# Re-ordering the opening of a diffusion-backbone kernel, the weight pieces of its last middle norm, and one convolution chunk

## The chip, the cores and the metric

The program runs on one core of a Trainium2 chip. The metric is the device time of one execution in microseconds (us). TensorE (PE in the profile) multiplies matrices, VectorE (DVE), ScalarE (ACT) and GpSimd (POOL) work elementwise, and SyncE (SP) issues transfers; ACT issues some transfers too. Each engine executes its own instructions in the order in which the program lists them and waits on semaphores where an operand is not there yet.

## The reference, cut to what matters

The reference is a two-layer trunk over 512 tokens of width 1024, all in float32:

```
h  = rmsnorm(x, g1) * (1 + s1) + sh1       # m = silu(c) @ w_mod + b_mod gives s1, sh1, ...
hc = the same for 256 context tokens, with silu(c_ctx)
layer 0: x += gate1 * mixer(h, hc)         # spatial gating beside neighbourhood attention, w_in / w_out
layer 1: x += gate1 * conv_module(h)       # pw1, GLU, 31-tap depthwise conv, layernorm, silu, pw2
both:    x += gate2 * (relu(rmsnorm(x, g2) * (1 + s2) + sh2) @ w1)^2 @ w2
out = rmsnorm(x, final_g)
```

Three places of it matter here. The **opening** is the first norm: sums of squares of x over the 1024 channels, the first quarter of the modulation vector of layer 0 (silu(c) and silu(c_ctx) times 2048 columns of `w_mod`), the modulated operand h, and the first query and key products with `w_in`. The **last middle norm** is the norm in layer 1 between the convolution module's output projection (pw2) and the MLP. The **convolution** works channel block by channel block.

## The kernel before, in words

Activations lie transposed, 128 channels on the partitions and 512 tokens along the free dimension, so x is eight blocks `x0[0..7]`. Every float32 operand of a large product is split in two float32r parts, hi (a rounded copy) and lo (the remainder), and each product is three matmuls: `w_hi·h_hi`, `w_lo·h_hi`, `w_hi·h_lo` (lines 88, 89 and 90, helper `mm3`). Weights come in tiles of 1024 x 256 (1 MB). A tile is cut into four **pieces** of two channel blocks each: ACT casts the hi part (line 93), DVE or POOL subtracts to get the lo part (line 94). `W.piece(i, q)` cuts piece q of weight i; `W.pieces(n)` cuts the next n; `W.use()` hands a cut weight out; cutting a weight's last piece issues the load of the next raw tile, which has two buffers.

The order of the work is written out by hand: the engines follow the program's order, and the program only adds the semaphores. Eight completion semaphores serve all transfers in turn.

**Opening (lines 246 to 524).** Transfers are issued first: SP takes `cc`, `x0[0,1]`, `x0[4,5]`, `vec`, `wmA0`, a raw weight, `wmA2`, `wmA3`, the second raw weight, `wmA4` to `wmA7`; ACT takes `x0[2,3]`, `x0[6,7]`, `kon`, `wmA1`. Then ACT computes `sc = silu(cc)` (line 370) while PE runs eight dummy products (`keep_warm`, line 376). ACT squares the eight x blocks (line 383), DVE adds them in pairs (line 385), and PE forms column sums of each pair with a vector of ones: four matmuls (eight instructions) per pair, line 387. The root follows (lines 391, 392). `mod_products(f)`, f = 0 to 3, makes modulation tile f: four products with `wmA[2f]`, four with `wmA[2f+1]` (line 421), an ACT copy `ms` (line 426), four transposes (line 430), and three small DVE operations (lines 435, 437, 438) that give gain and shift of x blocks 2f and 2f+1. `first_operand(f)` then makes hi (ACT, line 464) and lo (DVE, lines 465 and 466) of these two blocks. `first_products(ks, ns)` multiplies blocks ks with column groups ns of the first two weights; column groups 0 and 1 belong to weight 0, groups 2 and 3 to weight 1. In the kernel before, PE does the products of a block well after its operand was made: blocks 2 and 3 between modulation tiles 2 and 3, blocks 4 and 5 after tile 3. After blocks 6 and 7 the sums of squares of the context tokens are made (class `SumSq`: ACT squares at lines 310 and 313, DVE adds at line 321, one product with ones at line 327), and then the value products begin (line 88 with weight tile `w`).

**Convolution (conv_module, lines 1288 to 1437).** `glu(c)` multiplies a gate chunk and a value chunk and writes a padded row block `ypad` (DVE, line 1218); from it shifted copies `y4` are made by 16 transfers on SP (line 1242), for block 7 by 10 transfers and 6 ACT copies (line 1240). `conv_pe(c, t0, t1)` is the depthwise convolution of block c on PE (line 1262), 64 instruction pairs for half of the tokens. `take(c)` adds a finished block to the running sums. `W.pieces` and `work` put weight pieces and left-over vector work between.

**Last middle norm (norm_between, lines 1018 to 1100, called for this place by `lead1`).** PE finishes output chunks 4 and 5 over all tokens, then chunks 6 and 7 over the first 256 tokens, then chunk 6 over the second 256. In the middle of the last one stands the product with ones that totals the squares of the first half (line 327). DVE evacuates each chunk into x (line 1012), ACT squares it (line 313), DVE adds it (line 321). `chunk` puts its weight pieces ahead of its evacuation.

## Time and profile before

| | |
|---|---|
| median of 3 runs | 1176.19 us (1175.85 to 1176.26) |
| the profiled execution's own time | 1176.03 us |
| its span, first to last instruction | 1174.2 us |
| PE busy | 1154.7 us, 98% |
| DVE, ACT, POOL busy | 722.4, 473.9, 170.0 us |
| granted clock, mean over the span | 0.996 |

Matmul ends in the profile are modelled and matmuls overlap, so the time that PE loses is read from the starts of its instructions, and from the idle time that the profile puts ahead of one. "Idle before, <- X" names what ended the wait.

### The profile page before, as it was taken

To read this page: it belongs to the slowest core of one execution; us is meant where nothing else is said; L and a number is where in the kernel's file an instruction comes from. 1 tells how busy PE (TensorE), PEld (TensorE's weight loads), DVE (VectorE), ACT (ScalarE), POOL (GpSimd) and SP (SyncE) were. 2 spreads that over 40 slices of the span, in tenths; PEclk is the share of its full clock that TensorE was granted. 3 is DMA by queue.
4 is the path that set the end of the run, shared out by engine and by line. 5 is a ranking of instruction groups with operands and counts; after the bars stand their busy time and mean duration, and the time that the engine had idled before them with its cause. 6 is when DMAs were issued, how large, how long until landed. Compare 5 with 4: busy or idle time off the path is not lost.

```text
span 1174.2 us, 16562 instructions
## 1 busy us (share of the span) xinstructions
PE 1154.7 (98%) x6620; PEld 959.6 (82%) x6620; DVE 722.4 (62%) x1252; ACT 473.9 (40%) x939; POOL 170.0 (14%) x162
## 2 busy tenths in 40 slices
PE   8999999999999999999999999999999999999997
PEld 4688898889888888888889666698988888888887
DVE  4765778758765665666666878577643443443445
ACT  4474455546431422423336233564632331341423
POOL 0250327533000000000023110143200000000001
PEclk9999999999999999999999999999999999999999
DMA  9624543351554554554541444303232332232322
GB/s 383 228 81 137 188 162 109 126 215 37 215 210 152 212 215 156 203 215 172 186 144 41 151 113 140 99 24 122 72 107 73 108 108 77 103 108 72 108 73 72
DMA packets 31469, 161.91 MB, mean 138 GB/s; under 512 B 4320, under 2 KB 7904, under 8 KB 15008
## 3 DMA queue, kind: packets, MB, share of 16 engines
q1 hardware_dynamic: 27360, 146.09, 35.6%
q10 hardware_dynamic: 4032, 14.76, 3.7%
q8 instruction: 52, 0.85, 0.3%
q14 instruction: 25, 0.20, 0.1%
HBM read 152.52 MB, written 2.10 MB: 132 GB/s over the span
## 4 chain that ended last, share of the span: by engine, by line
PE 87%; DVE 6%; DMA 3%; ACT 2%; issue 1%; POOL 0%; ACTq 0%; DVEq 0%; SPq 0%; POOLq 0%
PE ps L88 23%; PE ps L90 22%; PE ps L89 22%; PE ps L214 4%; PE ps L211 4%; PE ps L212 4%; PE ps L1262 3%; PE ps L892 1%; DMA graw<-in_wmA_dram 1%; DVE graw L557 1%; DMA graw<-in_wmB_dram 1%; PE ps L846 1%; DVE acc L321 1%; PE ps L421 1%; PE ps L876 1%
## 5 line engine op out<-in xcount | busy, mean ns | idle before, releaser
L93 ACT CAST whi<-raw 128x512 fp32r<-128x512 f32 x340 | 191.2, 616 | 199.4 <-PE ps L90 152.3
L88 PE MATMUL ps<-hhi,whi 128*128 128x512 f32 x640 | 251.6, 393 | 1.4 <-DVE gn L743 1.4
L90 PE MATMUL ps<-hlo,whi 128*128 128x512 f32 x640 | 249.3, 390 | 0.6 <-DVE hlo L466 0.6
L89 PE MATMUL ps<-hhi,wlo 128*128 128x512 f32 x640 | 249.4, 390 | 0.2 <-DVE wlo L94 0.2
L94 DVE TENSOR_TENSOR wlo<-raw,whi 128x512 fp32r<-128x512 f32 x284 | 194.7, 723 | 35.6 <-ACT whi L93 34.7
L90 PE MATMUL ps<-hid,whi 128*128 128x512 f32 (+1 forms) x520 | 196.3, 378 | 0.0
L89 PE MATMUL ps<-hid,wlo 128*128 128x512 f32 (+1 forms) x520 | 196.3, 378 | 0.0
L88 PE MATMUL ps<-hid,whi 128*128 128x512 f32 (+1 forms) x520 | 196.3, 378 | 0.0
L1012 DVE SCALAR_TENSOR_TENSOR x<-ps,mod,x 128x512 f32<-128x512 f32 (+1 forms) x94 | 62.7, 668 | 156.8 <-PE ps L90 147.8
L88 PEld LDWEIGHTS ps<-hhi,whi 128*128 128x128 f32 x640 | 120.1, 188 | 32.4 <-issue 5.3
L94 POOL TENSOR_TENSOR wlo<-raw,whi 128x512 fp32r<-128x512 f32 x56 | 81.6, 1473 | 426.9 <-ACT whi L93 426.8
L90 PEld LDWEIGHTS ps<-hlo,whi 128*128 128x128 f32 x640 | 120.1, 188 | 26.1 <-DVE hlo L466 1.0
L89 PEld LDWEIGHTS ps<-hhi,wlo 128*128 128x128 f32 x640 | 120.2, 188 | 24.5 <-DVE wlo L94 0.5
L557 DVE CUSTOM_DVE_ANT_0 graw<-graw,cB,vec 128x1024 f32<-128x1024 f32 x80 | 107.4, 1345 | 15.8 <-DMA graw<-in_wmB_dram 15.8
L88 PEld LDWEIGHTS ps<-hid,whi 128*128 128x128 f32 x520 | 97.8, 188 | 18.2
L89 PEld LDWEIGHTS ps<-hid,wlo 128*128 128x128 f32 x520 | 97.8, 188 | 18.1
L90 PEld LDWEIGHTS ps<-hid,whi 128*128 128x128 f32 x520 | 97.8, 188 | 18.1
L1138 DVE TENSOR_TENSOR z<-z 128x512 f32<-128x512 f32 (+1 forms) x72 | 46.1, 646 | 95.5 <-ACT z L1136 95.5
L1136 ACT ACTIVATE z<-ps 128x512 f32<-128x512 f32 (+1 forms) x72 | 38.9, 550 | 140.6 <-PE ps L90 137.1
L1142 DVE TENSOR_TENSOR hid<-z,hid 128x512 fp32r<-128x512 f32 (+1 forms) x72 | 45.7, 641 | 43.3 <-ACT hid L1140 43.3
L1140 ACT CAST hid<-z 128x512 fp32r<-128x512 f32 (+1 forms) x72 | 40.6, 572 | 51.4 <-DVE z L1138 51.4
L1492 POOL TENSOR_TENSOR o<-o,rstd 128x256 f32<-128x256 f32 x2 | 1.9, 950 | 323.1 <-DVE rstd L332 323.1
(261 smaller groups left out, 1695.4 us busy)
## 6 DMA issues: line engine op xcount, KB each, us to landing
raw<-in_w_ff_dram SPq DMA_DIRECT2D x64, 1024.0 KB
graw<-in_wmB_dram SPq DMA_DIRECT2D x28, 1024.0 KB
graw<-in_wmB_dram ACTq DMA_DIRECT2D x24, 512.0 KB
raw<-in_w_pw_dram SPq DMA_DIRECT2D x12, 1024.0 KB
raw<-in_w_in_dram SPq DMA_DIRECT2D x10, 1024.0 KB
wmA<-in_wmA_dram SPq DMA_DIRECT2D x6, 1024.0 KB
y<-ypad SPq DMA_DIRECT2D x90, 67.5 KB
raw<-in_w_out_dram SPq DMA_DIRECT2D x4, 1024.0 KB
```

Of the source, the lines that this page charges most:

```text
L88: pe.matmul(ps, w[0], a[0], start=first, stop=False)
L89: pe.matmul(ps, w[1], a[0], start=False, stop=False)
L90: pe.matmul(ps, w[0], a[1], start=False, stop=last)
L93: (e or act.copy)(hi, src)
L94: (el or dve).tensor_tensor(lo, src, hi.bitcast(F32), op=ALU.subtract)
L211: pe.matmul(ps, w[0][:, k, c : c + P], a[0], start=n == 0, stop=False)
L212: pe.matmul(ps, w[1][:, k, c : c + P], a[0], start=False, stop=False)
L214: pe.matmul(ps, w[0][:, k, c : c + P], a[1], start=False, stop=n == len(ks) - 1)
L557: dve.tensor_tensor_reduce(out=wv, in0=wv, in1=cB, scale=1.0, scalar=vcol(V_BMOD, l * 48 + q * 8 + j % 8), op0=ALU.mult, op1=ALU.add, accu ...
L1012: dve.scalar_tensor_tensor(x[:, m, t0:t1], ps, gate[:, m : m + 1], x[:, m, t0:t1], op0=ALU.mult, op1=ALU.add)
L1138: dve.tensor_tensor(z, z, z, op=ALU.mult)
L1142: dve.tensor_tensor(lo, z, hi.bitcast(F32), op=ALU.subtract)
```

## The change

1. Opening, transfers. `wmA0` and `wmA1` are each cut in two halves, the first half issued by SP, the second by ACT; so ACT issues five transfers ahead of its first computation where it issued four. Of each of the first two raw weights only the first piece's share (two blocks, 256 KB) is loaded early, the rest after `wmA3`. `vec` moves behind the first share of raw weight 0. The two context loads move from the middle of the products to the end of this list.
2. Opening, sums. The Sqrt table is loaded ahead of the squares. ACT squares seven blocks in the order 0 to 5, 7; DVE squares block 6. Blocks 0+1, 2+3 and 7+6 are added in pairs, 4 and 5 are not: five groups of column sums where there were four.
3. Opening, products. `first_products` can issue only some of the three parts. Two of the three keep-warm dummies are gone. Modulation tiles and products come in a new order: block pair 2f, 2f+1 is multiplied directly after its operand is made, split in parts around the two halves and the transposes of the modulation tile. Weight pieces are cut one by one between. The copies of `cB` come after `first_operand(1)`. The context's squares and adds come ahead of the last products, their total in the middle of them, and the pieces of the third weight after the total.
4. Last middle norm, with `apart=True` for `lead1` alone: chunk 6's evacuation ahead of the weight pieces; one piece after it; after chunk 7's evacuation a flush of the sums and two pieces, one of them with POOL; the last piece after the second half of chunk 6.
5. Convolution: `conv_pe(5)` over the first half of the tokens moves from ahead of `glu(7)` to behind it.

```diff
     def load_wmA(i):
...
+        if i < 2:
+            sync.dma_start(w[:, :1024], I["wmA"][i][:, :1024])
+            act.dma_start(w[:, 1024:], I["wmA"][i][:, 1024:])
+        else:
+            sync.dma_start(w, I["wmA"][i])
...
-    vec = cp.tile([P, NV], F32, name="vec")
-    sync.dma_start(vec, I["vec"])
     kon = cp.tile([P, NC_], F32, name="kon")
     act.dma_start(kon[:, :C_MASK], I["kon"][:, :C_MASK])
     load_wmA(0)
     load_wmA(1)
-    W.load()
+    rest = [W.load(2)]
+    vec = cp.tile([P, NV], F32, name="vec")
+    sync.dma_start(vec, I["vec"])
+    rest.append(W.load(2))
     load_wmA(2)
     load_wmA(3)
-    W.load()
+    for go in rest:
+        go()
     for i in range(4, 8):
         load_wmA(i)
+    ctile = []
+    for k in range(0, KC, 4):
...
     keep_warm(8, 512)
+    preload(AF.Sqrt)
...
+    for k in (0, 1, 2, 3, 4, 5, 7, 6):
         sq = slot(s="sq")
+        if k == 6:
+            dve.tensor_tensor(sq, x0[k], x0[k], op=ALU.mult)
+        else:
+            act.activation(sq, x0[k], AF.Square)
+        sqs.append(sq)
+        if k in (1, 3, 6):
+            dve.tensor_tensor(sq, sq, sqs[-2], op=ALU.add)
+        if k in (1, 3, 4, 5, 6):
+            column_sums(sq, k == 1, k == 6)
-    preload(AF.Sqrt)
...
-    keep_warm(2, 256)
+    keep_warm(1, 256)
     run(pm)
     W.piece(0, 0)
+    wqk = {0: W.his[0]}
     first_operand(0)
...
+    first_products((0, 1), (0, 1), ("hh", "lh"))
+    pm = mod_products(1)
+    next(pm)
+    first_products((0, 1), (0, 1), hl)
+    W.piece(1, 0)
+    wqk[1] = W.his[1]
+    scaled(1)
+    next(pm)
+    first_products((0, 1), (2, 3), hh)
+    next(pm)
+    run(pm)
+    first_operand(1)
+    first_products((0, 1), (2, 3), ("lh", "hl"))
     for i in range(2):
         act.copy(cB[:, i * 512 : (i + 1) * 512], pbs[i])
...
+    W.piece(0, 1)
+    first_products((2, 3), (0, 1))
+    W.piece(1, 1)
+    scaled(2)
     pm = mod_products(2)
     next(pm)
+    first_products((2, 3), (2, 3), hh)
+    W.piece(0, 2)
     next(pm)
+    first_products((2, 3), (2, 3), lh)
+    next(pm)
     run(pm)
     first_operand(2)
+    first_products((2, 3), (2, 3), hl)
+    W.piece(0, 3)
+    first_products((4, 5), (0, 1))
+    W.piece(1, 2)
+    W.piece(1, 3)
...
     pm = mod_products(3)
     next(pm)
+    first_products((4, 5), (2, 3), hh)
     next(pm)
+    first_products((4, 5), (2, 3), lh)
+    next(pm)
     run(pm)
     first_operand(3)
+    first_products((4, 5), (2, 3), hl)
+    cs = SumSq()
+    for k in range(KC):
+        cs.add(ctile[k], 0, TC)
+    cs.flush()
+    first_products((6, 7), (0, 1))
+    cs.total(0, TC)
+    rc = cs.rstd(0, TC)
...
     W.pieces(4, pool)
-    first_products((6, 7))
...
+    first_products((6, 7), (2, 3))
...
-        chunk(6, w, 0, acts, evac, 0, ks, a0, a1, 3, "both")
+        if apart:
+            chunk(6, w, 0, acts, evac, 0, ks, a0, a1, 0)
+            W.pieces(1)
+        else:
+            chunk(6, w, 0, acts, evac, 0, ks, a0, a1, 3, "both")
         seven = together([(7, w, P)], acts, evac, a0, a1, ks)[0]
         seven()
+        if apart:
+            ss.flush()
+            W.pieces(1)
         W.pieces(1, pool)
...
         conv_weights(6)
-        conv_pe(5, a0, a1)
         take(4)
         glu(7)
         preload(AF.Silu)
         work(100)
+        conv_pe(5, a0, a1)
         conv_pe(5, b0, b1)
```

## The prediction

> **What bounds the kernel now.** I read the page first, then PE's waits, then the three places of the change in the timeline.

> ```profile
> PE 1154.7 (98%) x6620; PEld 959.6 (82%) x6620; DVE 722.4 (62%) x1252; ACT 473.9 (40%) x939; POOL 170.0 (14%) x162
> ```
> ```profile
> PE ps L327 <- DVE acc L321: 2.6, 2, 1.8
> PE ps L1262 <- DMA y<-ypad: 1.5, 2, 0.8
> ...
> PE ps L421 <- DMA graw<-in_wmA_dram: 1.2, 1, 1.2
> ...
> PE ps L430 <- ACT ms L426: 0.8, 1, 0.8
> ...
> PE ps L90 <- DVE hlo L466: 0.6, 1, 0.6
> ...
> PE ps L89 <- DVE wlo L94: 0.2, 1, 0.2
> ```

> PE bounds the whole span. Waits of PE are all that an edit of order can win, and the change aims at exactly these: the opening (L421, L430, L90, L89 and one L327), the last middle norm (the other L327), the convolution (L1262). Between them PE runs on, so what an early place wins or loses comes through to the end.

> **The opening, its start.** Here is what the transfers do, and ACT's and PE's first work:

> ```profile
> SPq L120 <- DMA x<-in_xT_dram: 2.3, 1, 2.3
> SPq L262 <- DMA cc<-in_cc_dram: 2.0, 1, 2.0
> SPq L262 <- DMA vec<-in_vec_dram: 1.9, 1, 1.9
> ```
> ```profile
> 3.28 1.28 ACT L370 ACT_TABLE_LOAD   x1 [3.28 <-issue]
> 4.88 0.42 ACT L370 ACTIVATE sc<-cc 128x256 f32<-128x256 f32 x1 [0.32 <-DMA cc<-in_cc_dram]
> 7.51 4.27 ACT L383 ACTIVATE sq<-x 128x512 f32<-128x512 f32 x8 [2.21 <-DMA x<-in_xT_dram]
> ...
> 8.70 0.69 DVE L385 TENSOR_TENSOR sq<-sq,sq 128x512 f32<-128x512 f32 x1 [8.70 <-ACT sq L383]
> ...
> 10.03 3.73 PE L387 MATMUL ps<-ones,sq 128*128 128x128 f32 x32
> ...
> 14.96 1.06 PE L421 MATMUL ps<-graw,sc 128*32 128x512 f32 x8 [1.19 <-DMA graw<-in_wmA_dram]
> ```

> SP's loads wait for landings that their data have nothing to do with: a weight waits for `x`, `wmA0` for `cc`. Counting issues over both queues, each transfer waits for the one eight before it. That is the eight semaphores in turn. Before, ACT issued only four early transfers, none beyond the eighth, and was never held.

> Now ACT issues five. Taking both queues in step, the order is cc, x0, x2, x4, x6, then `wmA0` first half, kon, `wmA0` second half, `wmA1` first half, `wmA1` second half. The last is the tenth, on ACT, and waits for the second, x block 0, which lands at 7.51 by the row of the squares. Everything ACT computes is queued behind it: table load, silu, the second table load that the change puts here, the squares. PE waits for the squares, DVE too.

> By the rows: 7.5 + 0.4 for the issue + 1.28 + 0.42 + 1.28 + 0.2 = 11.1 for the first square, against 7.51. A square takes 4.27/8 = 0.53; two are done at 12.2, their DVE add (0.69) at 12.95, and PE, idle since its dummies ended at 10.03, begins the column sums at 13.0. Five groups of eight at 3.73/32 = 0.117 each are 0.94 a group. The second pair is added at 14.0, and from there PE is the bound: 14.0 + 4 x 0.94 = 17.7. The first modulation product comes at 17.7 instead of 14.96: **2.7 later**. If ACT is not held, the table load fits into the 2.21 us in which ACT waited, and PE still needs 10.03 + 5 x 0.94 = 14.7, so the earlier landing of `wmA0` cannot bring more than 0.3. Bounds of this term: -0.3 and +2.7; I take the second, by the count.

> The other moves of transfers cost nothing. Second shares of the raw weights, `vec` and the contexts land late by their place in the list, but 14 MB at the rate of this row are in by 38, before the context's squares:

> ```profile
> 3.00:36.00 33.00, 30.24 (x154) 16.86 (x152) 18.86 (x41) 18.11 (x31) 0.00 (x0) 1.00 1.02 419
> ```

> The third and fourth raw tile are issued after about 45, and the value products need them after 55; a 1 MB tile takes 2.5 us at this rate. If that cover were gone it would be one such tile.

> **The opening, its products.** From 14.96 to the first value product at 55.17 PE needs 40.2 us:

> ```profile
> 20.52 1.03 PE L376 MATMUL ps<-ones 128*128 128x256 f32 x4
> ...
> 55.17 0.58 PE L88 MATMUL ps<-hhi,w 128*128 128x512 f32 x1
> ...
> 44.35:53.65 9.30, 9.30 (x43) 7.70 (x41) 8.52 (x9) 5.62 (x14) 5.87 (x4) 1.00 0.11 20
> ```

> A product takes 9.30/41 = 0.227 (41 weight loads). Removed are one dummy of the two in the first row, 0.5, a shorter one, 0.2 by its columns, and the waits 0.6 + 0.8 + 0.2 + 0.8 = 2.4. Work left: 37.1. What is added is waiting, because the new order multiplies a block pair directly behind its operand. The chain that makes one, with every link:

> ```profile
> 34.38 1.06 PE L421 MATMUL ps<-wmA,sc 128*32 128x512 f32 x8
> ...
> 35.52 0.59 ACT L426 COPY ms<-ps 128x512 f32<-128x512 f32 x1 [2.88 <-PE ps L421]
> ...
> 36.20 0.62 PE L430 MATMUL ps<-kon,ms 128*128 128x128 f32 x4
> ...
> 36.85 0.19 DVE L435 TENSOR_REDUCE modA<-ps 128x8 f32<-128x32 f32 x1 [0.97 <-PE ps L430]
> ...
> 37.48 1.52 ACT L464 ACTIVATE hhi<-x,modA,gsA 128x512 fp32r<-128x512 f32 x2 [1.38 <-DVE gsA L438]
> 38.33 0.55 DVE L465 TENSOR_SCALAR x<-x,gsA,modA 128x512 f32<-128x512 f32 x1 [0.88 <-ACT hhi L464]
> ...
> 38.91 0.69 DVE L466 TENSOR_TENSOR hlo<-x,hhi 128x512 fp32r<-128x512 f32 x1
> ```

> From the start of the second half of a modulation tile: 1.14 to the copy, 0.6 copy, 0.65 transposes, 0.63 small operations, 0.82 to the first hi: 3.85; to the first lo 1.3 more, 5.15. What PE has in between, tile by tile:

> - Tile 1: its second half 1.0, 4 products, transposes 0.45, 8 products: 4.2. The next product needs weight piece (0,1), whose cast stands on ACT behind the pair of hi and both `cB` copies: 3.85 + 0.76 + 1.06 + 0.6 = 6.3, its lo 0.7 later. Idle 2.1 and 0.5.

> ```profile
> 23.46 1.06 ACT L486 COPY cB<-ps 128x512 f32<-128x512 f32 x2
> ...
> 27.68 0.62 ACT L93 CAST whi<-raw 128x512 fp32r<-128x512 f32 x1
> ```

> - Tile 2: 1.0, 4 products, 0.45, 4 products: 3.3 against 3.85 and, after two products, 5.15. Idle 0.6 and 0.85.
> - Tile 3: the same, 1.45. Behind it the context's seven adds (0.41 each undisturbed, as in the norm below, 0.36 from start to start) follow the second lo: 3.85 + 4 x 0.6 + 7 x 0.36 = 8.8, and PE is through with its ten products at 5.15 + 2.3 = 7.45. Idle 1.3.
> - Tile 0: its first hi comes when the one dummy left is over; 0.6 in two waits.

> Sum 7.4, so 44.5 against 40.2: **4.3 longer**. Each duration is a row's; the bounds are 2 (more than half of the waits filled by work that I set too early) and 5.5. In the kernel before these chains cost almost nothing: tile 2 is made while products of blocks 0 to 2 last, and blocks 4 and 5 come after tile 3.

> **The clock.** PE's granted clock fell once, behind a wait:

> ```profile
> 804.97:806.88 1.91, 0.15 (x2) 0.00 (x0) 1.65 (x4) 1.28 (x3) 0.00 (x0) 1.00 0.00 0
> 807.40:810.70 3.30, 3.30 (x16) 3.21 (x16) 2.35 (x3) 0.55 (x2) 0.83 (x1) 0.50 0.44 112
> ```

> After 1.9 us without matmuls it was 0.50 for 3.4 us, in which 16 products took 3.3 instead of 16 x 0.12 = 1.9: a loss of 1.4. Two gaps of this kind come new: 3.0 us (10.03 to 13.0) and 2.6 us (tile 1). A gap of 2.4 in the convolution below left the clock at 1.0, and one of 1.35 before 14.96 too. Each new gap costs 0 to 1.4. Both are longer than the one that halved the clock, so I take most of both bounds: 2.0 in all.

> [...]

> **The last middle norm.** PE comes to the total at 804.97 and gets it at 806.88:

> ```profile
> 802.07 0.69 DVE L94 TENSOR_TENSOR wlo<-raw,whi 128x512 fp32r<-128x512 f32 x1 [1.69 <-ACT whi L93]
> 803.11 1.36 DVE L94 TENSOR_TENSOR wlo<-raw,whi 128x512 fp32r<-128x512 f32 x1 [0.35 <-ACT whi L93]
> 804.40 0.47 DVE L1012 SCALAR_TENSOR_TENSOR x<-ps,mod,x 128x256 f32<-128x256 f32 x1
> ...
> 806.40 0.42 DVE L321 TENSOR_TENSOR acc<-acc,sq 128x256 f32<-128x256 f32 x1 [0.21 <-ACT sq L313]
> ```

> Chunk 6's evacuation at 804.40 stood behind two weight pieces whose raw tile had just landed; its matmuls ended at 800.5 (24 at 0.12 between 797.4 and 800.3). Evacuated first, chunk 6 is in x at 801.0, one piece fits in (802.1 to 802.8), chunk 7 ends at 803.3, evacuation 803.8, square 804.25, flushed add 804.7: ahead of 804.97. The wait of 1.9 goes, and with it the halved clock, 1.4, and slow totals, 0.2: **-3.5**. What is late next is the reciprocal (it can start at 806.0) and the first hi, at 808.6, where PE comes with its next products at 809.2. Bounds -1.5 (a piece lands in the new way) to -3.5; I take -3.5.

> **The convolution.** PE's last block waits for shifted copies:

> ```profile
> 737.19 0.75 DVE L1218 SCALAR_TENSOR_TENSOR ypad<-ps,vec,sg 128x512 f32<-128x512 f32 x1 [1.38 <-PE ps L90]
> ...
> 738.00 7.05 SPq L1242 DMA_DIRECT2D y<-ypad  x10
> ...
> 743.96 0.59 PE L1262 MATMUL ps<-y,cB 128*32 128x256 f32 x2
> 745.39 0.59 PE L1262 MATMUL ps<-y,cB 128*32 128x256 f32 x2 [0.84 <-DMA y<-ypad]
> 746.62 3.43 PE L1262 MATMUL ps<-y,cB 128*32 128x256 f32 x58 [0.64 <-DMA y<-ypad]
> ```

> Four instructions at 3.43/58 = 0.06 took 2.66. Moving 64 pairs (3.5 us) behind `glu(7)` brings its end, and `ypad`, forward by up to 3.5; DVE, which has takes and a piece in front of it, allows about 2.4. So the copies land at 744.2 and the wait is nearly gone: **-2.2**, between -1 and -2.4.

> **The sum.** 2.7 + 4.3 + 2.0 - 3.5 - 2.2 = +3.3 on the profiled execution's own 1176.03, which stands 0.16 under the median shown: 1179.5 on that median.

> **Rivals.**
> 1. *ACT is not held*, or only for `cc`, which lands before 4.88 and costs 1 us at most: the tenth transfer is another one. For it: how the issues of two queues interleave is not in the trace. The start is then within 0.3 of before and its gap is gone: 0 + 4.3 + 1.2 - 5.7 = -0.2: 1176.0. No change.
> 2. *The parts cover the chain: faster.* PE finds the operands in the opening, because ACT's casts run ahead of tile 1's chain and work that I set too early fills the waits of tiles 2 and 3; start as in rival 1, added idle time 3.7 less: 0 + 0.6 + 0 - 5.7 = -5.1: 1171.1. It decides from an opening that costs under 3.3. Against it: the cast of piece (0,1) is written behind both copies, and each link of the chain is a row.
> 3. *The late wins are eaten* while the forecast's opening holds: SP issues its ten copies at 0.7 each whenever they start, and the norm's first hi comes late. 9.0 - 1.5 - 1.0 = +6.5: 1182.7.

> **How the numbers follow.** Forecast 0.50, rival 1 0.25, rival 2 0.15, rival 3 0.10. A change under 0.2% (2.35 us) is not told from none: faster means under 1173.8, slower over 1178.5. The forecast's own range is 1177.2 (its products at their low bound) to 1182; four fifths of it lie over 1178.5, and rival 3 wholly: 0.50. Rival 2 and a tail of rival 1 are faster: 0.18. The rest is 0.32. The range leaves out the ends of rivals 2 and 3: 1173.2 to 1182.8.

> **What the changed profile would show.** ACT's first table load near 7.9 and its squares near 11.1 show the hold (near 3.3 and 7.5: rival 1). The first L421 near 17.7, and the first value product near 63, show the opening's sum; idle times ahead of L88 and L90 of 2, 0.5, 0.6, 0.85 the chains. No idle time ahead of the norm's L327, clock 1.0 behind it, and no L1262 wait for `y` show the late wins. An opening that reaches the value products before 58.5 would make the prediction wrong.

## The result, and the profile after

| | before | after |
|---|---|---|
| median (4 runs each) | 1176.13 us | 1184.99 us (1184.59 to 1185.37) |
| ratio, 95% interval | | 1.0076 [1.0058, 1.0093] |
| the profiled execution's own time | 1176.03 us | 1185.37 us |
| its span | 1174.2 us | 1183.6 us |

The kernel became slower by 0.76%, 8.9 us. The forecast had the sign, but its 1179.5 was 5.5 us short, and the result lies 2.2 us above the range.

Where the 9.3 us between the two profiled executions arose is read from instructions that both have. After, in the timeline of PE (start, busy time, instruction):

```profile
13.26 6.36 PE L402 MATMUL ps<-ones,sq 128*128 128x128 f32 x40 [2.14 <-DVE sq L414]
19.55 1.06 PE L447 MATMUL ps<-graw,sc 128*32 128x512 f32 x8
...
69.00 0.39 PE L88 MATMUL ps<-hhi,w 128*128 128x512 f32 x1
...
757.04 4.57 PE L1307 MATMUL ps<-y,cB 128*32 128x256 f32 x62
...
765.21 1.05 PE L1395 MATMUL ps<-ones,lsum 128*128 128x1 f32 x8
...
1175.00 0.38 PE L1548 MATMUL ps<-ones,sq 128*128 128x1 f32 x2 [0.60 <-ACT sq L330]
```

The last two of these in the kernel before:

```profile
753.65 0.49 PE L1350 MATMUL ps<-ones,lsum 128*128 128x1 f32 x3
...
1165.71 0.38 PE L1503 MATMUL ps<-ones,sq 128*128 128x1 f32 x2 [0.60 <-ACT sq L313]
```

With the rows that the prediction shows of before (10.03, 14.96, 55.17, 743.96) the changed kernel is behind by 3.23 at the column sums, 4.59 at the first modulation product, **13.83 at the first value product**, 13.08 at the last block of the convolution, 11.56 at the sums behind it, and 9.29 at the end. The opening costs 13.8 where 9.0 were forecast; the convolution gives back 1.52 (2.2 forecast), the norm 2.27 (3.5 forecast), and 0.75 goes in the attention and the first MLP, where nothing was edited.

PE's waits after (us in total, times, longest):

```profile
PE ps L344 <- DVE acc L338: 2.7, 2, 2.2
PE ps L402 <- DVE sq L414: 2.1, 1, 2.1
PE ps L483 <- ACT whi L93: 1.9, 1, 1.9
PE ps L483 <- ACT hhi L494: 1.4, 3, 0.6
...
PE ps L483 <- DVE hlo L496: 1.2, 2, 0.6
```

L402 is the opening's start, the rows of L483 are products that now stand directly behind their operand or weight, 2.2 of L344 is the context's total. The other 0.46 of L344 and a wait of 0.30 for the first hi (L217) are new waits of the last middle norm.

ACT in the opening:

```profile
7.85 0.33 ACTq L270 DMA_DIRECT2D wmA<-in_wmA_dram  x1
8.22 1.28 ACT L387 ACT_TABLE_LOAD   x1 [8.22 <-DMA x<-in_xT_dram]
...
9.95 1.28 ACT L308 ACT_TABLE_LOAD   x1
...
11.35 3.73 ACT L411 ACTIVATE sq<-x 128x512 f32<-128x512 f32 x7
```

ACT's fifth issue goes out at 7.85, when x has landed, and the first square stands at 11.35.

The granted clock is the column behind the five engines' busy times; each pair of rows is a stretch with a long wait and the stretch behind it:

```profile
10.47:13.88 3.41, 1.27 (x7) 0.62 (x6) 1.02 (x2) 3.40 (x7) 0.00 (x0) 1.00 1.01 390
13.88:17.29 3.41, 3.41 (x18) 3.41 (x18) 1.75 (x3) 1.20 (x3) 0.00 (x0) 0.50 1.02 385
34.36:37.77 3.41, 1.12 (x5) 0.50 (x4) 3.34 (x6) 3.12 (x6) 0.00 (x0) 1.00 0.76 304
37.77:41.19 3.42, 3.42 (x10) 2.64 (x9) 2.00 (x4) 0.00 (x0) 0.00 (x0) 0.50 0.02 8
61.67:65.08 3.41, 1.18 (x6) 0.85 (x5) 1.93 (x5) 0.20 (x1) 0.00 (x0) 1.00 0.00 0
65.08:68.49 3.41, 3.41 (x9) 2.69 (x9) 3.07 (x2) 2.34 (x5) 2.56 (x3) 0.50 0.00 0
```

All three long waits of the opening are followed by 3.4 us at half speed. In the profiled execution of the kernel before, the clock fell only once ahead of the end, in the norm.

### The profile page after: what moved, and what is told of

Its sections match the earlier page's. It is cut to its first block, busy times and chain, and to the rows that moved or that the text cites. A ratio compares the mean times of both kernels' runs of the same rounds, so it can differ in the third digit from the quotient of the medians.

```text
span 1183.6 us, 16573 instructions
## 1 busy us (share of the span) xinstructions
PE 1160.8 (98%) x6624; PEld 961.9 (81%) x6624; DVE 722.8 (61%) x1253; ACT 473.3 (40%) x938; POOL 167.0 (14%) x161
## 5 line engine op out<-in xcount | busy, mean ns | idle before, releaser
L93 ACT CAST whi<-raw 128x512 fp32r<-128x512 f32 x340 | 191.3, 616 | 197.9 <-PE ps L90 152.6
L88 PE MATMUL ps<-hhi,whi 128*128 128x512 f32 x608 | 238.4, 392 | 1.4 <-DVE gn L779 1.4
L89 PE MATMUL ps<-hhi,wlo 128*128 128x512 f32 x608 | 236.7, 389 | 0.0
L90 PE MATMUL ps<-hlo,whi 128*128 128x512 f32 x608 | 236.7, 389 | 0.0
L94 DVE TENSOR_TENSOR wlo<-raw,whi 128x512 fp32r<-128x512 f32 x285 | 195.0, 721 | 33.4 <-ACT whi L93 27.0
L90 PE MATMUL ps<-hid,whi 128*128 128x512 f32 (+1 forms) x520 | 196.3, 378 | 0.0
L89 PE MATMUL ps<-hid,wlo 128*128 128x512 f32 (+1 forms) x520 | 196.3, 378 | 0.0
L88 PE MATMUL ps<-hid,whi 128*128 128x512 f32 (+1 forms) x520 | 196.3, 378 | 0.0
L94 POOL TENSOR_TENSOR wlo<-raw,whi 128x512 fp32r<-128x512 f32 x55 | 79.0, 1450 | 428.8 <-ACT whi L93 428.7
L88 PEld LDWEIGHTS ps<-hhi,whi 128*128 128x128 f32 x608 | 114.1, 188 | 28.1 <-issue 3.2
L90 PEld LDWEIGHTS ps<-hlo,whi 128*128 128x128 f32 x608 | 114.1, 188 | 24.0
L89 PEld LDWEIGHTS ps<-hhi,wlo 128*128 128x128 f32 x608 | 114.2, 188 | 23.0
L89 PEld LDWEIGHTS ps<-hid,wlo 128*128 128x128 f32 x520 | 97.8, 188 | 18.3
L90 PEld LDWEIGHTS ps<-hid,whi 128*128 128x128 f32 x520 | 97.8, 188 | 18.1
L88 PEld LDWEIGHTS ps<-hid,whi 128*128 128x128 f32 x520 | 97.8, 188 | 18.0
```

The lines of the kernel that those rows point to most:

```text
L88: pe.matmul(ps, w[0], a[0], start=first, stop=False)
L89: pe.matmul(ps, w[1], a[0], start=False, stop=False)
L90: pe.matmul(ps, w[0], a[1], start=False, stop=last)
L93: (e or act.copy)(hi, src)
L94: (el or dve).tensor_tensor(lo, src, hi.bitcast(F32), op=ALU.subtract)
```

## Experiments

Ratios are to the kernel before, run beside each on the same chip; its medians there were 1174.5 to 1176.0 us, its single executions 1172.7 to 1178.6.

**1. The late edits alone.**

```diff
 # kernel before, with the changed norm_between(..., apart=True) and
-        conv_pe(5, a0, a1)
         take(4)
         glu(7)
...
+        conv_pe(5, a0, a1)
         conv_pe(5, b0, b1)
```

> The kernel before with the edits of the last middle norm and the convolution alone; the opening stays as it was. Theory 1: these two edits are worth what the aligned traces show, 1.5 us and 2.3 us, whatever the opening does: 1172.3 us, and the first value product stays at 55.2. Theory 2: the waits come back elsewhere once the opening does not hide them (the gain of 3.8 was a shift of the 3.4 us stretches of the clock): 1175 to 1177 us.

Measured: 1172.36 us, ratio 0.9963 [0.9950, 0.9976]. Its first value product is at 55.19. Theory 1 holds: the late edits win 0.37% by themselves, so the whole loss is the opening's. The two were then run one by one.

> The kernel before with the edit of the last middle norm alone. Theory 1: the wait of 1.8 ahead of the total and the halved clock behind it go, two new waits (0.3 ahead of the next first hi, 0.46 ahead of the second total) come: 2.3 us less, ratio 0.998, and no execution shows a halved clock near 807. Theory 2: the forecast's 3.5 us: ratio 0.997, no new waits.

Measured: 1174.33 us, ratio 0.9984 [0.9975, 0.9994]; in the profiled execution no clock fall near 807, and the same two new waits (0.30 and 0.45). Theory 1 in the waits; the interval just leaves out the forecast's 0.997. By the medians the gain is 1.6 and not 2.3. The fall that the edit takes away does not come in every execution with the old norm: it is absent from the profiled executions of the convolution alone (next) and of the two halves (experiment 3). That this makes the difference was not tested.

> The kernel before with the edit of the convolution alone. Theory 1: the ten copies of block 7 leave 2.5 us earlier against the work of PE, but follow the next raw weight directly and take 0.8 us each instead of 0.7, so 0.7 us of the wait stays: 1.5 us less, ratio 0.9987. Theory 2: the forecast's 2.2 us, no wait left: ratio 0.998.

Measured: 1174.37 us, ratio 0.9987 [0.9977, 0.9996]. The size is theory 1's, but the profiled execution (1174.21) does not bear out how it came about. There the convolution gave back only 0.4 (its sums start at 753.27, before at 753.65), and most of the rest is the fall of the clock in the norm, which did not come in this execution (last section). The copies took longer still than theory 1 says, and the queue's row says why:

```profile
734.62 0.33 SPq L120 DMA_DIRECT2D raw<-in_w_pw_dram  x1
735.32 9.36 SPq L1242 DMA_DIRECT2D y<-ypad  x10
```
```profile
SPq L1242 <- DMA raw<-in_w_pw_dram: 2.3, 1, 2.3
```

SP holds the copies back for 2.3 us until the raw weight that was issued 0.7 us ahead of them has landed. The copies do not need that weight. Between the seventh copy (740.04) and the eighth (742.9) lies the whole wait: the eighth copy is the eighth transfer behind the weight. It is the count of the opening again. In the trace of the kernel before, all 278 transfers end on one of eight semaphores, 34 or 35 on each. SP's wait is 0.3 in the changed kernel (ten copies in 8.15 instead of 7.05) and absent where the edits were run together, so how much of the gain arrives seems to depend on how fast 1 MB lands in that execution; this was not tested.

**2. The clock.** The three waits filled with dummies:

```diff
-    keep_warm(8, 512)
+    keep_warm(10, 512)
...
     first_products((0, 1), (2, 3), ("lh", "hl"))
+    keep_warm(2, 512, bank())
...
+    keep_warm(2, 512, bank())
     cs.total(0, TC)
```

> The changed kernel with six dummy products more: two of 512 columns after the first eight, two after the last products of blocks 0 and 1, two ahead of the context's total. They depend on nothing, compute nothing that is used, and fill PE's idle time of 2.1, 1.9 and 2.2 us there. Theory 1: each of these idle times made the clock fall to 0.50 for 3.4 us, and each fall costs some 1.6 us of work at half speed: without them the opening is 3 to 5 us shorter although PE does 5.8 us more work, 1180 to 1182 us, and no stretch at 0.50 stays ahead of the end. Theory 2: the falls cost nothing of note, because PE waits there for other engines anyway: 1185 us, or above it where a dummy is in the way of a product.

Measured: 1182.0 us, ratio 1.0051 [1.0036, 1.0066], 3.0 us less than the changed kernel although PE does more. No stretch ahead of the end is at half speed, and the mean granted clock is 0.997 against 0.993:

```profile
13.88:17.29 3.41, 3.41 (x32) 3.34 (x31) 1.73 (x3) 1.18 (x3) 0.00 (x0) 1.00 1.07 399
```
```profile
18.05 1.06 PE L447 MATMUL ps<-graw,sc 128*32 128x512 f32 x8
...
64.36 0.39 PE L88 MATMUL ps<-hhi,w 128*128 128x512 f32 x1
```

In this stretch PE starts 32 matmuls here and 18 in the changed kernel. The first modulation product comes 1.5 earlier (18.05 against 19.55), the first value product 4.6 earlier (64.36 against 69.00). So the falls cost 4.6 in the opening: theory 1. Part of that is lost again further on, 1.6 by the medians and 2.8 in the profiled execution (1183.53, the slowest of four). There PE waits 1.3 at 89.8 for the low part of the attention keys, which DVE makes behind twelve small multiplications. These took twice as long as in the changed kernel, whose row is the last:

```profile
81.44 7.96 DVE L763 TENSOR_TENSOR biases<-rows,kon 128x128 f32<-128x128 f32 x12
85.04 4.21 POOL L94 TENSOR_TENSOR wlo<-raw,whi 128x512 fp32r<-128x512 f32 x3 [0.26 <-ACT whi L93]
```
```profile
83.52 3.60 DVE L761 TENSOR_TENSOR biases<-rows,kon 128x128 f32<-128x128 f32 x12
```

Five of the twelve last 1.35 to 1.38 instead of 0.28: each starts while POOL subtracts a weight piece (1.3 to 1.5) and ends 0.15 behind it. In the changed kernel with four transfers on ACT (experiment 3) one of the twelve is caught, and there is no such wait. A further 0.7 goes at the convolution's copies.

**3. ACT's hold.** First the hold put into the kernel before, then taken out of the changed one:

```diff
 # kernel before
-        (act if i == 1 else sync).dma_start(w, I["wmA"][i])
+        if i < 2:
+            sync.dma_start(w[:, :1024], I["wmA"][i][:, :1024])
+            act.dma_start(w[:, 1024:], I["wmA"][i][:, 1024:])
+        else:
+            sync.dma_start(w, I["wmA"][i])
```

> The kernel before with the two halves of the first two modulation tiles alone (second halves issued by ACT, which so issues five transfers ahead of its first computation). Theory 1: ACT's fifth issue waits for block 0 and 1 of x and goes out at 7.9; first table load at 8.2, first square near 10 instead of 7.5, PE's first column sum near 12 and the first modulation product near 16 instead of 15.0; 1 us more, and 1.5 us more than that where the idle time halves the clock: 1177 to 1179 us. Theory 2: ACT's hold needs the rest of the list's new order: table load at 3.3, 1175 to 1176 us.

Measured: 1175.27 us, ratio 0.9996 [0.9986, 1.0006]. The hold is there, but its cost is too small to show in the time. ACT's fifth issue goes out at 7.59, the first square stands at 9.57, the first modulation product at 15.69 instead of 14.96, 0.7 later. I had expected a fall of the clock too, but the wait ahead of the column sums is only 1.0 long. Here PE no longer waits for the first modulation tile (1.19 before), and the second table load still stands behind the squares, at 13.84. With that load ahead of them and five groups of sums the hold costs 3.1 (experiment 2: 18.05 against 14.96).

The same execution shows something about the clock that the forecast had wrong. The norm's wait ahead of its total was 2.24 long here, longer than the 1.76 that halved the clock in the kernel before, and the clock did not fall. Cut at this execution's stretches, it is 1.24 idle in the one and 1.00 in the other:

```profile
801.08:804.49 3.41, 2.17 (x19) 1.97 (x17) 3.06 (x6) 1.02 (x3) 1.29 (x1) 1.00 0.30 123
804.49:807.91 3.42, 2.42 (x18) 2.37 (x19) 1.85 (x3) 1.40 (x3) 1.28 (x1) 1.00 0.09 12
```

```diff
 # changed kernel
-            act.dma_start(w[:, 1024:], I["wmA"][i][:, 1024:])
+            (act if i == 0 else sync).dma_start(w[:, 1024:], I["wmA"][i][:, 1024:])
```

> The changed kernel with the second half of the second modulation tile issued by SP, so that ACT issues four transfers as it did before. Theory 1: ACT is not held, its first table load is at 3.3 and its squares start near 7.5; PE's first column sum comes near 10.5 without idle time, the clock does not fall at 13.9, and the first modulation product comes at 15 to 16 instead of 19.6: 4 us less, 1181 us. Theory 2: the fourth issue is held as well, or the squares wait for x to nearly the same time: 1184 to 1185 us.

Measured: 1180.45 us, ratio 1.0038 [1.0025, 1.0050], 4.5 less than the changed kernel. ACT's first table load is at 3.06, the squares at 7.66:

```profile
3.06 1.28 ACT L387 ACT_TABLE_LOAD   x1 [3.06 <-issue]
```
```profile
15.26 1.07 PE L447 MATMUL ps<-graw,sc 128*32 128x512 f32 x8
```

One issue moved to the other queue is half of the whole loss (3.1 of hold and its 1.5 of clock). Rival 1 of the prediction had the right price for the start in this case (within 0.3 of before: 15.26 against 14.96); its whole sum, 1176.0, is 4.5 too low, since the products and the clock cost more and the late edits win less.

**4. What is left of the opening.** The next three start from the changed kernel with four transfers on ACT.

```diff
     for i in range(2):
         act.copy(cB[:, i * 512 : (i + 1) * 512], pbs[i])
 # moved behind
     W.piece(0, 1)
     first_products((2, 3), (0, 1))
     W.piece(1, 1)
```

> The changed kernel with four transfers on ACT, and with the two copies of cB moved from ahead of weight piece (0,1) to behind weight piece (1,1). Theory 1: in the wait of tile 1 (1.9 and 0.4 us) 1.04 us are the two copies, so it falls to 0.8 and 0.4, and what is left no longer halves the clock (1.6 us): 1180.45 less 2.6 is 1177.8 us. Theory 2: the cast waits for its raw weight or for the pair of hi in any case: the same wait, 1180 to 1181 us.

Measured: 1180.58 us, ratio 1.0045 [1.0030, 1.0060]: no gain. Theory 2 in the time, but by another way than it said:

```profile
30.67 0.49 PE L483 MATMUL ps<-hhi,whi 128*128 128x512 f32 x1 [0.89 <-ACT whi L93]
...
32.56 0.65 PE L483 MATMUL ps<-hhi,wlo 128*128 128x512 f32 x1 [1.39 <-DVE wlo L94]
```

The cast comes 1 us sooner, as it should, and the wait for its low part grows from 0.42 to 1.39, because DVE makes that low part only behind both operands' low parts. The sum stays 2.28, within one stretch, and the clock falls as before. Two queues stood behind the tile; I had unblocked one.

```diff
     first_products((6, 7), (0, 1))
-    cs.total(0, TC)
-    rc = cs.rstd(0, TC)
...
     W.pieces(4, pool)
     first_products((6, 7), (2, 3))
+    cs.total(0, TC)
+    rc = cs.rstd(0, TC)
```

> The changed kernel with four transfers on ACT, and with the context's total and root behind the last twelve products of blocks 6 and 7 instead of ahead of them. Theory 1: the twelve products (2.7 us) cover the context's adds, the idle time of 2.2 us and the halved clock behind it (1.6 us) go: 1180.45 less 3.8 is 1176.7 us. Theory 2: POOL cuts the third weight beside the adds and makes each of them longer (0.8 instead of 0.5 us in the kernel before), so part of the wait stays: 1178 to 1179 us.

Measured: 1181.84 us, ratio 1.0056 [1.0039, 1.0073]: above both theories, in the way that theory 2 names.

```profile
55.93 7.27 DVE L338 TENSOR_TENSOR acc<-acc,sq 128x256 f32<-128x256 f32 x7
...
57.39 5.53 POOL L94 TENSOR_TENSOR w<-raw,w 128x512 fp32r<-128x512 f32 x4 [56.37 <-ACT w L93]
...
63.35 0.67 PE L344 MATMUL ps<-acc,ones 128*128 128x256 f32 x2 [3.18 <-DVE acc L338]
```

Beside POOL's four subtractions an add takes 1.04. The wait is 3.18, twelve more products ahead of it notwithstanding. In the changed kernel the pieces stand behind the total, and the adds are half as long:

```profile
60.43 3.59 DVE L338 TENSOR_TENSOR acc<-acc,sq 128x256 f32<-128x256 f32 x7
```

So the changed order pays for short adds with a wait of 2.2 in PE; the kernel before makes the adds beside POOL too (0.80 each), but under 24 products. By the rows an add takes 0.51 alone and 1.04 beside subtractions of 1.38 (5.53/4); what makes it longer was not tested.

```diff
     first_products((0, 1), (2, 3), ("lh", "hl"))
+    keep_warm(2, 512, bank())
...
+    keep_warm(2, 512, bank())
     cs.total(0, TC)
```

> The changed kernel with four transfers on ACT and two dummy products of 512 columns in each of two places: after the last products of blocks 0 and 1, and ahead of the context's total. Theory 1: with ACT free and the clock kept, only the waits of the chains and PE's slower restart behind each of them are left of the opening's cost: some 6 us above the kernel with both late edits alone (1172.36), 1177 to 1178.5 us, no fall of the clock. Theory 2: the forecast's 4.3 us were right and the rest of the difference is something the falls hide: 1176.5 us or less.

Measured: 1179.54 us, ratio 1.0039 [1.0024, 1.0055], outside both theories. The opening does what theory 1 says: first value product at 61.19, 3.5 earlier than with four transfers on ACT alone (64.72) and 6.0 behind the kernel before. But the keys' low part is now 1.6 late, again behind twelve multiplications stretched to 7.97 beside POOL. In the profiled execution (1181.32) that wait makes the clock fall in its turn:

```profile
84.12:87.54 3.42, 1.81 (x14) 1.40 (x14) 3.04 (x7) 2.29 (x6) 1.73 (x2) 1.00 0.42 123
87.54:90.95 3.41, 3.41 (x14) 2.25 (x11) 2.62 (x9) 1.89 (x5) 0.00 (x0) 0.50 1.02 260
```

The median is not an execution with this fall: the three at 1179.5 had a mean granted clock of 0.997 or 0.998, the profiled one 0.996 and the slowest (1182.97) 0.995. The wait alone, on top of theory 1's 1177 to 1178.5, would be enough for 1179.5.

**5. A kernel that beats both.** Four steps from the late edits; the first two:

```diff
-    vec = cp.tile([P, NV], F32, name="vec")
-    sync.dma_start(vec, I["vec"])
...
     load_wmA(1)
     W.load()
+    vec = cp.tile([P, NV], F32, name="vec")
+    sync.dma_start(vec, I["vec"])
```

> The kernel before with both late edits, and with vec issued behind the first raw weight, so that the first modulation tile is the seventh transfer and not the ninth. Theory 1: it no longer waits for a semaphore of an earlier transfer, the 0.8 to 1.2 us ahead of the first modulation product go and nothing else moves: 1172.36 less 1.0 is 1171.3 us. Theory 2: the tile lands no sooner, because the transfers ahead of it fill the queues: 1172.4 us.

Measured: 1171.39 us, ratio 0.9965 [0.9954, 0.9977], 1.0 below the late edits alone by the medians, not told apart by the ratios. The wait ahead of the first modulation product falls from 0.82 to 0.3 in the profiled executions.

```diff
-    first_products((0, 1), (0, 1))
+    first_products((0,), (0, 1))
+    first_products((1,), (0,))
     pm = mod_products(1)
     next(pm)
     next(pm)
+    first_products((1,), (1,))
     next(pm)
...
-                    if c == 7 and 4 * g + u > 9:
+                    if c == 7 and 4 * g + u > 7:
...
-        if apart:
-            W.pieces(1)
         seven = together([(7, w, P)], acts, evac, b0, b1, ks)[0]
         W.free()
         go(ma_, 2)
+        if apart:
+            W.pieces(1)
```

> The kernel before with both late edits and vec later, and three more: three products of blocks 0 and 1 between the second half of modulation tile 1 and its transposes (there PE waits 0.76); the third weight piece of the last middle norm two steps later (there two new waits of 0.3 and 0.46); eight instead of six of block 7's shifted copies on ACT, two fewer on SP (there some 0.7 are left of the wait). Theory 1: the waits go, 1171.3 less 1.9 is 1169.4 us. Theory 2: only the first goes; the norm's wait moves to another piece, and ACT, two copies of 0.65 longer, is late with its own next work: 1170.6 to 1172 us.

Measured: 1169.82 us, ratio 0.9957 [0.9942, 0.9971]. The waits of 0.76 (modulation tile 1) and 0.3 (norm's first hi) are gone, that of the second total is 0.27. By the waits and the median it is theory 1, nearly all of it; the ratios do not tell this step from the one before.

```diff
     first_operand(2)
+    cs = SumSq()
+    for k in range(4):
+        cs.add(ctile[k], 0, TC)
     first_products((2,), (3,))
...
-    cs = SumSq()
-    for k in range(KC):
+    for k in range(4, KC):
         cs.add(ctile[k], 0, TC)
```

> The kernel with both late edits, vec later and the three further edits (1169.82), with the squares and adds of context blocks 0 to 3 made behind the operand of tile 2, where DVE waits for modulation tile 3. Theory 1: only four adds are left beside POOL's work on the third weight, they end ahead of the last product of blocks 6 and 7, the wait of 0.8 ahead of the total goes: 1169.0 us. Theory 2: the adds make tile 3's small operations late and PE waits there instead: 1169.8 us or more.

Measured: 1173.02 us, ratio 0.9980 [0.9969, 0.9991], slower than without it. Theory 2 has the place, modulation tile 3, but not the cause: the adds were not what was late. ACT waited for the context itself, and modulation tile 3 behind it on ACT:

```profile
ACT acc L310 <- DMA ctx<-in_ctxT_dram: 4.9, 1, 4.9
...
PE ps L430 <- ACT ms L426: 3.0, 1, 3.0
```

So the last one takes from the change what it did for these transfers, the context loads at the end of the opening's list:

```diff
     for i in range(4, 8):
         load_wmA(i)
+    ctile = []
+    for k in range(0, KC, 4):
+        t = mpa.tile([P, 4, TC], F32, tag="ablk", name=nm("ctx"), bufs=6)
+        sync.dma_start(t, I["ctxT"][:, k : k + 4, :])
+        ctile += [t[:, i] for i in range(4)]
...
     first_operand(1)
     for q in range(1, 4):
         W.piece(1, q)
-    ctile = []
-    for k in range(0, KC, 4):
-        t = mpa.tile([P, 4, TC], F32, tag="ablk", name=nm("ctx"), bufs=6)
-        sync.dma_start(t, I["ctxT"][:, k : k + 4, :])
-        ctile += [t[:, i] for i in range(4)]
```

> The kernel with the late edits, vec later, the three further edits and the first four context adds early (1173.0), with the two context loads issued at the end of the opening's list, behind the modulation tiles, where the changed kernel has them. Theory 1: in the run before, only the data were late (ACT waited 4.9 us for the context and PE 3.0 for modulation tile 3 behind it); landed by 36, they cost nothing, the fall of the clock there goes, and the 0.8 us ahead of the total go too: 1169.0 us. Theory 2: the loads, 1 MB ahead of the third raw weight, make that weight late instead: 1171 us or more.

Measured: **1167.82 us, ratio 0.9936 [0.9918, 0.9954]**, the fastest, though its interval overlaps that of the three further edits [0.9942, 0.9971]. The squares start at 37.36 without a wait, and the total no longer waits:

```profile
52.41 0.59 PE L332 MATMUL ps<-acc,ones 128*128 128x256 f32 x2
```

The first value product, at 52.66, is 2.5 ahead of the kernel before. The change's early context loads were worth having here; its order of products was not.

## Why the prediction was wrong, point by point

| term | forecast | measured | from |
|---|---|---|---|
| start of the opening, clock left out | +2.7 | +3.1 | 18.05 with the waits filled, 14.96 before |
| products, clock left out | +4.3 | +6.1 | 64.36 - 18.05 = 46.3, against 40.2 |
| clock | +2.0 | +4.6 | 69.00 - 64.36 |
| last middle norm | -3.5 | -2.3 | 11.56 to 9.29 |
| convolution | -2.2 | -1.5 | 13.08 to 11.56 |
| elsewhere | 0 | -0.75 | 13.83 to 13.08, cause not settled |

**Start: right.** The tenth transfer waits for x, as the count of issues said; forecast and row differ by 0.25 at the first square (11.1, 11.35) and at the column sums (13.0, 13.26). Taking the fifth issue away gave back 4.5, and rival 1's "not held" did not happen.

**Products: mechanism and waits right, one term left out.** The waits were forecast as 7.4 in sum. Here they are, with the steps behind them:

```profile
36.49 0.50 PE L483 MATMUL ps<-hhi,whi 128*128 128x512 f32 x1 [1.86 <-ACT whi L93]
37.41 0.50 PE L483 MATMUL ps<-hhi,wlo 128*128 128x512 f32 x1 [0.42 <-DVE wlo L94]
...
42.70 1.20 PE L483 MATMUL ps<-hhi,whi 128*128 128x512 f32 x4
43.83 1.07 PE L447 MATMUL ps<-wmA,sc 128*32 128x512 f32 x8
...
47.98 0.50 PE L483 MATMUL ps<-hhi,whi 128*128 128x512 f32 x1 [0.60 <-ACT hhi L494]
48.32 0.40 PE L483 MATMUL ps<-hhi,wlo 128*128 128x512 f32 x1
49.29 0.50 PE L483 MATMUL ps<-hlo,whi 128*128 128x512 f32 x1 [0.58 <-DVE hlo L496]
...
64.17 0.67 PE L344 MATMUL ps<-acc,ones 128*128 128x256 f32 x2 [2.23 <-DVE acc L338]
```

Tile 1 has 1.86 and 0.42 (forecast 2.1 and 0.5), tiles 2 and 3 0.60 and 0.58 each (0.6 and 0.85), the context's total 2.23 (1.3). Tile 0 had 0.24 (0.6). Together 7.1. What failed is the step "Work left: 37.1". It keeps all products at the pace of the kernel before, 0.227 in an undisturbed run; the work measured is 46.3 less 7.1, so 39.2. The first product behind a wait takes 0.34 (47.98 to 48.32), and a group of four between modulation products 1.13 (42.70 to 43.83) instead of 4 x 0.227 = 0.91. The change cuts the products into such groups and puts seven long waits between them. The missing 2.1 is of the size of these restarts, and they are the only places that I found; it was not tested by itself.

**Clock: the term that failed.** I had two gaps, each 0 to 1.4, and took 2.0 of the 2.8. There were three falls, 1.5 to 1.6 each. The third gap was in the forecast too, at 1.3 us, less than the 1.60 of idle time that left the clock at 1.00 (last section); it was 2.2. And the price was a matter of either-or, not of a share: in each of the three rows the whole stretch of 3.41 us is at 0.50. The "gap of 2.4" in the convolution, which the forecast took for a long wait that left the clock alone, was two waits of 0.84 and 0.64 with products between them.

**Norm: mechanism right, one neighbour missed.** The wait of 1.76 and the half-speed stretch are gone. The forecast named the reciprocal and the first hi as the next late steps and found them early enough. The step that failed is "one piece fits in" for the third piece: it went ahead of the next multiplication on DVE,

```profile
822.38 0.81 DVE L94 TENSOR_TENSOR wlo<-raw,whi 128x512 fp32r<-128x512 f32 x1 [1.20 <-ACT whi L93]
823.12 0.87 DVE L363 SCALAR_TENSOR_TENSOR t<-x,gs,rstd 128x256 f32<-128x256 f32 x2
```

and cost PE 0.30 at the next hi and 0.46 at the second total; with PE's restart behind each (0.31 to the next product at 828.18, 0.12 further on), that is the 1.2 between forecast and measurement. Moved two steps on, as part of the fifth experiment, the first of these went and the second fell to 0.27.

**Convolution: size off.** The padded block was made, and its copies left, 2.6 earlier against the products that need them (`ypad` starts 9.37 ahead of them instead of 6.77), near the 2.4 of the forecast. The step that failed is that their own time stays 7.05: it became 8.15 behind the raw weight. Rival 3 had said that SP would eat a part of the win, for another reason.

**The chances.** The sign was right for the right reason. The range ended at 1182.8, the forecast's own at 1182. Even the upper bounds of the opening's three terms (2.7, 5.5 and 2 x 1.4) add up to 11.0, and 13.8 were measured: the clock's bound was too low by a whole fall, the products' by what I take for the restarts. The premise that what an early place loses comes through to the end held here within 0.75; it did not hold for the run with the dummies, where 2.8 of the 4.6 won were lost again. Rival 2, the faster opening, had nothing in the runs for it: each of its chains waited. Of the signs that the forecast named, the hold, the idle times of the chains and the norm's first total came as written; the first modulation product (17.7 forecast, 19.55) and the first value product (63, 69.0) were later by the falls and, as I take it, the restarts.

## What to carry to other kernels

Where PE is the bound, count its idle time by stretch of the clock and not by wait: here 1.61 of 3.41 us idle was enough for the next 3.41 us to run at 0.50, and filling such waits with products that nobody uses won 3.0 us (1182.0 against 1185.0). Keep older products beside the chain that makes the next operand; multiplying directly behind the operand made the opening's products 6.1 us longer with the clock left out (waits of 7.1, and 0.34 instead of 0.227 for the first product behind a wait), and 3.1 more by two falls of the clock. And count transfers over all queues by eights before adding or moving one: here waiting for the one eight before held ACT for 5 us in one place (first table load at 8.22 instead of 3.06) and SP for up to 2.3 in another, for data that neither needed.

## What the runs showed of the hardware

```profile
803.92:807.33 3.41, 1.65 (x14) 1.42 (x12) 2.70 (x6) 1.34 (x3) 0.38 (x2) 1.00 0.02 7
807.33:810.75 3.42, 3.42 (x18) 3.33 (x17) 2.40 (x3) 0.60 (x2) 0.90 (x1) 0.50 0.42 108
```

The longest without a fall in these two was 1.44 (before, from 192.93). The two nearest to the border: in the row at 84.12 above PE was idle for 1.61 and the clock fell, and in the convolution-alone kernel it was idle for 1.60 and did not:

```profile
804.96:808.37 3.41, 1.81 (x13) 1.76 (x14) 1.84 (x5) 1.44 (x4) 1.28 (x1) 1.00 0.00 0
808.37:811.78 3.41, 3.41 (x31) 3.41 (x30) 3.37 (x7) 1.57 (x4) 0.00 (x0) 1.00 0.84 283
```

So a wait of about 2 us made the clock fall or not by where it lay in the grid: ahead of the norm's total 1.76 did in the kernel before, and 2.24, cut into 1.24 and 1.00, did not in the kernel with the two halves. The ends of matmuls are modelled, so the border between 1.60 and 1.61 is not exact, and it is not all that counts: in the last 25 us, where PE runs products of a single column, the clock fell in nine of the executions behind a stretch with only 0.72 to 1.26 us of idle time. What else counts there is open.

**A VectorE operation or a GpSimd operation was longer beside the other.** A multiplication of 0.28 lasted 1.35 to 1.38 where it started during a POOL subtraction of 1.3 to 1.5, and ended 0.15 behind it. Elsewhere POOL's operation is the longer one: in the kernel before one of its subtractions lasted 2.47 (from 73.17; the mean of all 56 is 1.47) while DVE multiplied at 0.28 each. How many multiplications were stretched differed with how the work of the two lay: one of twelve with four transfers on ACT, five of twelve in both kernels with dummies. That made the keys late by 1.3 and 1.6 there, in one profiled execution with a fall of the clock of its own. Why was not tested.
